# A matmul with rotary embedding on one core: the lower rows follow the upper rows at 1024 columns, in another order of the banks

## The chip, the cores and the metric

One core of one Trainium2 chip. TensorE (PE) multiplies and transposes, VectorE (DVE), ScalarE (ACT) and GpSimd (POOL) work on tensors, and SyncE (SP), ScalarE and GpSimd issue DMA transfers. The metric is the device time of one execution in microseconds; less is better. Each engine works through its instructions in order and waits on semaphores that others raise.

## The reference

```
y = np.matmul(x, weight)                       # x: (16, 512, 768), weight: (768, 768)
y = y.reshape(batch, seq, n_heads, head_dim)   # 12 heads of 64
y1, y2 = y[..., :32], y[..., 32:]
out1 = y1 * cos1 - y2 * sin1                   # cos, sin: (512, 64), by place in the sequence
out2 = y2 * cos2 + y1 * sin2
out = np.concatenate([out1, out2], axis=-1).reshape(batch, seq, hidden)
```

All inputs and the output are float32. The kernel multiplies in float16 and accumulates in float32.

## The kernel before

**Tiles, pairs, groups.** The 8192 rows of `x` are 64 tiles of 128 rows. Four tiles make a group (`QB` = 4, 16 groups, `g`), two make a pair. A group takes the same places of the sequence from four batches, so that one slice of the cosine and sine table serves it. Its result has 4 x 768 = 3072 columns, and these lie in PSUM as `py`, six banks of 512 float32 columns (`ps0` to `ps5`). A pair has 1536 columns, three banks, and the border between its two tiles lies in the middle of the second of them.

**The way of a tile.** SyncE loads it (`load`, line 192), ScalarE casts it to float16 (`cast`, 227), TensorE transposes its six chunks of 128 x 128 into PSUM (`turn`, 235, or `turn_rows`, 247, which does it in two halves of 64 rows), and ScalarE copies that to SBUF as `xt` (the copy in the same function). From group 5 to 14 the second pair of each group comes another way: it is loaded as blocks (`load_quarter`, 200), by SyncE and then cast by ScalarE (`cast_pair`, 265), or by GpSimd's queue, which casts on the way, and VectorE transposes it (`turn_pair`, 273) into `xp`. The weight is loaded and cast once at the start.

**Upper and lower rows.** A tile's product needs six chunks of the contraction. In the groups 1 to 14 each chunk is split in two matmuls: one on the upper 64 rows of the TensorE array (`r` = 0) and one on the lower 64 (`r` = 1), which run at the same time. Both halves add into the same bank of PSUM. The function `steps` (330) cuts a tile into three steps of 256 output columns (six chunks, 1536 streamed columns); where a whole bank belongs to one tile, two steps are done as matmuls of 512 columns, three chunks each. `both` (359) puts a step `n` of the upper rows beside step `n - LAG` of the lower rows, with `LAG` = 3 (587), in the order of streamed columns. So the lower rows are one tile behind, and are in another bank. The upper rows' first matmul opens a bank (`start`), and the first lower one waits by semaphore for the upper rows' last in that bank (`closed`, `after`). When the lower rows have finished a bank, its rope is emitted.

**The rope.** `rope` (379) works on units of `units` (292). VectorE multiplies a unit's columns in PSUM by the cosines and by the sines and writes both products to SBUF (line 394); GpSimd adds them, with the halves of each head swapped in the second (410), to the output tile `ov`. In the groups 1 to 13 VectorE takes 512 columns and GpSimd 1024, two units together. The products lie in five buffers of 2 x 1024 columns: `tq` (three) and two in the memory of the raw weight, which is free after its cast. Group 0 has units of 1024 columns and is multiplied with all 128 rows (`mm_piece`, 319); so is the last group (15), which has three units of 512 and six of 256, of which VectorE adds the last two itself (`late`).

**Order.** All is written out by hand in the loop of line 605, tile by tile: the matmuls with their ropes, a transpose of a tile three ahead, the casts five ahead, GpSimd's loads twenty ahead, and the stores. `turns` and `casts` go in line with the other work of TensorE and ScalarE. A group's output is stored by two transfers that ScalarE issues after the first (`s` = 0) and the third tile (`s` = 2) of the next group (633 to 636). `Flow.do` (42) records for each instruction what it reads and writes, and puts in the semaphore waits that follow from it. After the loop's end the last group's pieces are stored, by SyncE and ScalarE.

Of the kernel before, what the change touches and what calls it, by code (L numbers as in the profile page):

```python
# [10 lines left out]
FP32 = mybir.dt.float32  # L11
# [94 lines left out]
def kernel(  # L106
# [37 lines left out]
    NX, NB, NBH, NC, NCP, NXT, NXP, NTQ, NOV = 10, 3, 3, 5, 2, 8, 4, 3, 4  # L144
# [14 lines left out]
    tq_b = [sbuf(f"tq{i}", [P, 2, 1024], FP32) for i in range(NTQ)]  # L159
    w_flat = w_raw.rearrange("p t e n -> p (t e n)")  # L160
    tq_b += [w_flat[:, ts(i, 2048)].rearrange("p (j n) -> p j n", j=2) for i in range(2)]
    W_HOME = [f"wr{t}{h}" for t, h in CHUNKS]
    ov_b = [sbuf(f"ov{i}", [P, QB * H], FP32) for i in range(NOV)]
# [128 lines left out]
    def units(g):  # L292
        if g == 0:
            return [(c, c + 1024, py[:, c : c + 1024], [f"ps{c // 512}", f"ps{c // 512 + 1}"], "pool")
                    for c in (0, 1024, 2048)]
        u = [(c, c + 512, py[:, c : c + 512], [f"ps{c // 512}"], "pool")
             for c in range(0, 3072 if g < LAST else 1536, 512)]
        if g == LAST:
            for k, (home, bank) in enumerate([
                (py[:, 1536:1792], "ps3"), (py[:, 0:256], "ps0"),  # L300
                (py[:, 2048:2304], "ps4"), (py[:, 2560:2816], "ps5"),
                (pt_b[0][:, 0:256], "pt0"), (pt_b[1][:, 0:256], "pt1"),
            ]):
                c = 1536 + 256 * k
                u.append((c, c + 256, home, [bank], "pool" if k < 4 else "dve"))
        return u
# [20 lines left out]

    closed = {}

    def steps(n, r):  # L330

        i, part = divmod(n, 3)
        g, s = divmod(i, QB)
        c0 = s * H + 256 * part
        bank, wide = c0 // 512, (s % 2 == 0 and part < 2) or (s % 2 == 1 and part > 0)
        lo = bank * 512 if wide else c0
        hi = lo + (512 if wide else 256)
        first, final = c0 % 512 == 0, c0 % 512 == 256
        chunks = (CHUNKS[:3] if first else CHUNKS[3:]) if wide else CHUNKS
        rows = ts(r, HP)  # L340
        get, key = xT[i]
        out_ = []
        for t, h in chunks:
            opens = r == 0 and first and (t, h) == chunks[0]
            shuts = final and (t, h) == chunks[-1]

            def go(t=t, h=h, opens=opens, shuts=shuts):
                after = closed[g, bank] if r and first and (t, h) == chunks[0] else 0
                do("pe", lambda eng: eng.matmul(  # L349
                    py[:, lo:hi], get(t, h)[rows], w_sb[rows, t, h, lo - s * H : hi - s * H],  # L350
                    start=opens, stop=r == 1 and shuts, skip_group_check=True),
                    reads=[key, f"w{t}{h}"], writes=[f"ps{bank}"], tick=shuts, after=after)
                if r == 0 and shuts:
                    closed[g, bank] = f.count["pe"]

            out_.append((hi - lo, go))
        return out_, (g, bank) if r == 1 and final else None

    def both(n, m):

        done, work = None, []
        for r, k in ((0, n), (1, m)):
            if k is None:
                continue
            mm, ended = steps(k, r)
            done = ended or done
            at = 0
            for cols, go in mm:
                work.append((at, r, len(work), go))
                at += cols  # L370
        for _, _, _, go in sorted(work, key=lambda w: w[:3]):
            go()
        return done
# [5 lines left out]
    def rope(g, u):  # L379
# [3 lines left out]
        half = 0 < g < LAST - 1  # L383
        if adder == "dve":
            k = len(late)
            tq, keys = xs_b[k][:, 0 : 2 * w].rearrange("p (j n) -> p j n", j=2), [f"xs{k}"]
        elif half and c0 % 1024:
            k = tq_of[0]
            tq, keys = tq_b[k][:, :, w : 2 * w], [f"tq{k}b"] + (W_HOME if k >= NTQ else [])
        else:  # L390
            k = tq_of[0] = ring("tq", NTQ + 2)
            tq = tq_b[k][:, :, 0:w]
            keys = [f"tq{k}a"] + [f"tq{k}b"] * (not half) + (W_HOME if k >= NTQ else [])
# [10 lines left out]
        if half:  # L404
            if c0 % 1024 == 0:
                return
            c0, w, tq, keys = c0 - w, 2 * w, tq_b[k], [f"tq{k}a", f"tq{k}b"]
# [179 lines left out]
    LAG = 3  # L587

# [16 lines left out]
    for i in range(QB, NTILE):  # L605
# [4 lines left out]
        if g < LAST:  # L610
            for n in range(3 * i, 3 * i + 3):
                done = both(n, n - LAG if n - LAG >= 3 * QB else None)
                if done:
                    rope(done[0], units(done[0])[done[1]])
                if n == 3 * i and i > QB + 1:
                    turns(i + T_AHEAD, 1)
        for n in range(3 * i - LAG, 3 * i) if i == QB * LAST else ():
            done = both(None, n)
            if done:
                rope(done[0], units(done[0])[done[1]])  # L620
# [12 lines left out]
        if s == 0 and g > 0:  # L633
            store(g - 1, 0, 2 * H, "act")
        if s == 2 and g > 0:
# [50 lines left out]
```

## Time and profile before

| | |
|---|---|
| median of 3 runs (range) | 154.4 us (154.16 to 154.4) |
| the profiled execution: its time | 154.73 us |
| its span, first to last instruction | 152.9 us |
| mean granted TensorE clock | 0.994 |
| a lower or upper 512-column matmul, by the modelled duration | 0.376 us, x672 |
| a 256-column one | 0.269 us, x672 |
| VectorE rope of 512 columns (x51 in `tq`) | 1.215 us |
| VectorE rope of 1024 columns (group 0) | 2.285 us |
| VectorE transposes of a pair | 0.969 and 1.235 us |
| ScalarE cast of a tile, copy of a transposed tile | 0.902 and 0.799 us |
| GpSimd add of 1024 columns | 2.373 us |

Matmuls are pipelined, so their durations overlap in one row half; the distance between their starts is what a matmul costs. The rope's shape is given in the profile as 128x1024 where it writes two products of 512 columns each. The chain of waits follows the last instruction back to what released it; an engine that is not on it costs nothing there. "py" is the product in PSUM, "pt" the PSUM of the transposes, "xc" a cast tile.

### The profile page before, as it was taken

The page shows a single profiled execution, that of the slowest core. Times are in us where ns is not written, and L with a number is a line of the kernel's source. Part 1 is how long each engine was busy: PE and PEld are TensorE (multiplying, and loading weights), DVE is VectorE, ACT ScalarE, POOL GpSimd, SP SyncE. Part 2 cuts the span into 40 slices and gives each one's busy share as a digit, 9 for nine tenths or more (in the row PEclk, how much of TensorE's full clock was granted, in tenths as well). Part 3 has the DMA queues.
Part 4 walks back from the last instruction along what each step waited for, and adds up shares of the span by engine and source line. Part 5 has one row for each costly group of instructions (what it writes and reads, how often), then busy time and mean ns, then how long its engine had stood idle before and what let it go on. Part 6 is the DMA issues. An engine that isn't in the chain of part 4 may idle for free.

```text
span 152.9 us, 4416 instructions
## 1 busy us (share of the span) xinstructions
PE 141.5 (93%) x1944; PEld 102.7 (67%) x1944; DVE 129.3 (85%) x119; ACT 78.7 (51%) x92; POOL 124.6 (81%) x81
## 2 busy tenths in 40 slices
PE   6669997999999999999999999999999999999930
PEld 2325674777777778777777777777777777766720
DVE  0244995888888999999999999999999999978980
ACT  3444778879778843556263726273526735461000
POOL 1000299599999999999999999999997979799970
PEclk9999999999999999999999999999999999999997
DMA  3999999999999999999999999999999998550992
GB/s 124 350 395 404 400 402 385 385 380 257 363 358 352 368 336 353 349 400 340 339 341 392 364 336 339 372 370 334 345 360 407 416 403 323 233 210 0 374 354 97
DMA packets 27555, 51.27 MB, mean 335 GB/s; under 512 B 7184, under 2 KB 13072, under 8 KB 27536
## 3 DMA queue, kind: packets, MB, share of 16 engines
q1 hardware_dynamic: 13504, 24.78, 46.8%
q10 hardware_dynamic: 8592, 24.25, 40.3%
q0 software_dynamic: 5440, 1.97, 10.4%
q8 instruction: 15, 0.25, 0.6%
q14 instruction: 4, 0.03, 0.1%
HBM read 27.79 MB, written 25.17 MB: 346 GB/s over the span
## 4 chain that ended last, share of the span: by engine, by line
PE 86%; DMA 5%; DVE 3%; SPq 1%; ACT 1%; issue 1%; DVEq 0%
PE py L349 72%; PE py L324 8%; DMA w_raw<-in_weight_dram 5%; PE pt L257 4%; PE pt L242 1%; DVE w_raw L394 1%; SPq L196 1%; DVE ov L410 1%; SPq L218 1%; ACT xc L176 1%; ACT xt L176 1%; DVE xs L394 0%; DVE w_sb L176 0%; DVE tq L394 0%; DVEq L57 0%
## 5 line engine op out<-in xcount | busy, mean ns | idle before, releaser
L349 PE MATMUL py<-w_sb,xt 64*128 64x512 f16 (+1 forms) x864 | 95.6, 323 | 0.0
L410 POOL TENSOR_TENSOR ov<-tq 128x1024 f32<-128x1024 f32 (+2 forms) x33 | 68.9, 2109 | 19.3 <-DVE tq L394 19.1
L394 DVE TENSOR_TENSOR tq<-py,csn 128x1024 f32<-128x1024 f32 (+2 forms) x56 | 68.1, 1253 | 3.6 <-PE py L349 3.1
L349 PEld LDWEIGHTS py<-w_sb,xt 64*128 64x128 f16 x864 | 58.8, 94 | 17.2
L349 PE MATMUL py<-w_sb,xp 64*128 64x512 f16 (+1 forms) x480 | 61.9, 323 | 0.0
L176 ACT COPY xt<-pt 128x768 f16<-128x768 f16 x42 | 33.5, 799 | 39.4 <-PE pt L257 27.3
L176 ACT CAST xc<-xs 128x768 f16<-128x768 f32 x44 | 39.1, 902 | 21.1 <-DMA xs<-in_x_dram 17.2
L394 DVE TENSOR_TENSOR w_raw<-py,csn 128x1024 f32<-128x1024 f32 (+1 forms) x38 | 45.3, 1191 | 5.3 <-PE py L349 3.7
L410 POOL TENSOR_TENSOR ov<-w_raw 128x1024 f32<-128x1024 f32 (+2 forms) x22 | 44.3, 2027 | 3.4 <-DVE w_raw L394 3.2
L349 PEld LDWEIGHTS py<-w_sb,xp 64*128 64x128 f16 x480 | 35.5, 94 | 9.9
L324 PE MATMUL py<-w_sb,xt 128*128 128x256 f16 (+1 forms) x96 | 15.5, 313 | 1.9 <-DVE w_sb L176 1.7
L257 PEld LDWEIGHTS pt<-ident,xc 64*128 64x128 f16 x432 | 13.7, 95 | 2.7 <-ACT xc L176 1.4
L324 PEld LDWEIGHTS py<-w_sb,xt 128*128 128x128 f16 x96 | 8.7, 98 | 7.5 <-DVE w_sb L176 3.2
L257 PE MATMUL pt<-ident,xc 64*128 64x64 f16 x432 | 12.6, 190 | 1.1 <-ACT xc L176 1.1
L211 POOL DMA_DIRECT2D xh<-in_x_dram x20 | 11.7, 594 | 0.0
L176 ACT CAST xd<-xb 128x1536 f16<-128x1536 f32 x5 | 8.2, 1630 | 1.5 <-DMA xb<-in_x_dram 1.4
L176 DVE CAST w_sb<-w_raw 128x768 f16<-128x768 f32 x6 | 3.4, 560 | 4.4 <-DMA w_raw<-in_weight_dram 4.4
L285 DVE STREAM_TRANSPOSE xp<-xh 128x768 f32<-128x768 f32 x5 | 6.2, 1235 | 0.0
L492 PE MATMUL py<-cold 128*128 128x512 f16 x12 | 4.3, 518 | 1.4 <-DVE cold L435 1.4
L176 DVE COPY xt<-pt 128x768 f16<-128x768 f16 x2 | 1.1, 557 | 4.9 <-PE pt L242 4.9
L285 DVE STREAM_TRANSPOSE xp<-xd 128x768 f32<-128x768 f32 x5 | 4.8, 969 | 0.0
L242 PEld LDWEIGHTS pt<-ident,xc 128*128 128x128 f16 x48 | 3.0, 98 | 2.7 <-ACT xc L176 1.8
(16 smaller groups left out, 13.2 us busy)
## 6 DMA issues: line engine op xcount, KB each, us to landing
out_dram<-ov ACTq DMA_DIRECT2D x30, 768.0 KB, 8.8
xs<-in_x_dram SPq DMA_DIRECT2D x44, 384.0 KB, 15.9
xb<-in_x_dram SPq DMA_DIRECT2D x20, 192.0 KB, 18.0
w_raw<-in_weight_dram SPq DMA_DIRECT2D x6, 384.0 KB, 7.8
xh<-in_x_dram POOLq DMA_DIRECT2D x20, 96.0 KB, 13.7
out_dram<-ov SPq DMA_DIRECT2D x1, 384.0 KB, 3.1
out_dram<-ov ACTq DMA_DIRECT2D x1, 384.0 KB, 2.8
out_dram<-ov SPq DMA_DIRECT2D x1, 256.0 KB, 2.1
```

What stands on the lines that cost most here:

```text
L176: eng.copy(out=o, in_=i_) if e == "act" else eng.tensor_copy(out=o, in_=i_)
L196: do(e, lambda eng: eng.dma_start(out=xs_b[k], in_=x[b].rearrange("(p r) h -> r p h", r=SB)[r]), writes=[f"xs{k}"], dma=f"xs{k}")
L211: do(e, lambda eng: eng.dma_start(out=dst[ts(q, R)], in_=src[r, q]), writes=[f"{name}q{q}"], dma=name)
L218: do(e, lambda eng: eng.dma_start(out=w_raw[:, t, h], in_=wv[t, h]), writes=[f"wr{t}{h}"], dma=f"w{t}{h}")
L242: do("pe", lambda eng: eng.transpose(pt[:, t, h, :], src[:, t, h, :], ident), reads=[f"xc{c}", "ident"], writes=[f"pt{k}"], tick=(t, h) == ...
L257: do("pe", lambda eng: eng.transpose(pts[r][:, t, h, :], src[rows, t, h, :], ident[rows, rows]), reads=[f"xc{c}", "ident"], writes=[f"pt{r ...
L285: do("dve", lambda eng: eng.transpose(out=dst, in_=src), reads=rd, writes=[f"xp{z}"])
L324: do("pe", lambda eng: eng.matmul(ps, get(t, h), w_sb[:, t, h, a - s * H : z - s * H], start=start, stop=stop), reads=[key, f"w{t}{h}"], w ...
L349: do("pe", lambda eng: eng.matmul(py[:, lo:hi], get(t, h)[rows], w_sb[rows, t, h, lo - s * H : hi - s * H], start=opens, stop=r == 1 and s ...
L394: do("dve", lambda eng: eng.tensor_tensor(out=tq.rearrange("p j (h d) -> p j h d", d=D), in0=ps.rearrange("p (h d) -> p h d", d=D) .unsque ...
L410: do(adder, lambda eng: eng.tensor_tensor(out=ov_b[o][:, ds(c0, w)].rearrange("p (h t d) -> p h t d", t=2, d=HD), in0=tq[:, 0].rearrange(" ...
L492: do("pe", lambda eng: eng.matmul(py[:, ts(b, 512)], cold[:, 0:P], cold, start=True, stop=warmed[0] < WARM - 6), reads=["cold"], writes=[f ...
```

## The change

The upper rows take a pair's three banks in the order 0, 1, 2 as before. The lower rows now take them in the order 2, 0, 1, and start 1024 streamed columns (two matmuls of 512) behind the upper rows (`LAG` = 1024), not one tile. Bank 2 is therefore opened by the lower rows and closed by the upper ones, the banks 0 and 1 the other way round. A bank's columns are done for all six chunks before the next, and the middle bank in two parts of 256 columns. `walk` yields this order for a pair and one half of the rows, `one` emits a matmul, and the new `both` merges the two lines by their streamed columns. The pair's second tile is so needed by the lower rows 1024 columns after the pair begins.

A rope is emitted when all of its banks have been finished by both halves. In the groups 1 to 14 a pair has a unit of 512 columns (its first bank) and one of 1024; GpSimd adds 1536 columns at once in the groups 1 to 13. The buffers of the products are one memory of 6144 columns and the raw weight's 4608, cut by `products` into three homes for a pair's 2 x 1536 columns, into three of 2 x 1024 for group 0 and six of 2 x 512 for the last group. Stores of the groups 0 to 13 are issued one tile later in the next group; those of group 14 are where they were.

```diff
+    tq_mem = sbuf("tq", [P, 6144], FP32)
+    def products(at, n, lo, hi):
+        mem, base, name = (tq_mem, at, "tq") if at < 6144 else (w_flat, at - 6144, "tw")
...
+    HOMES0, HOMES, HOMESL = (0, 2048, 4096), (6144, 0, 3072), (0, 1024, 2048, 3072, 4096, 5120)
...
+        if g < LAST:
+            return [(c, z, py[:, c:z], [f"ps{b}" for b in range(c // 512, z // 512)], "pool")
+                    for c, z in ((0, 512), (512, 1536), (1536, 2048), (2048, 3072))]
...
-    LAG = 3
+    LAG = 1024
...
+    def walk(pair, r):
+        g, h = divmod(pair, 2)
+        for bank in ((0, 1, 2) if r == 0 else (2, 0, 1)):
+            opens = (r == 0) == (bank < 2)
+            lo = h * 1536 + bank * 512
+            parts = [(lo, lo + 512)] if bank != 1 else [(lo, lo + 256), (lo + 256, lo + 512)]
+            for a, z in parts:
+                i = g * QB + a // H
+                for c in CHUNKS:
+                    yield z - a, (g, i, a, z, r, c, opens,
+                                  opens and (a, c) == (lo, CHUNKS[0]),
+                                  c == CHUNKS[-1], z == lo + 512)
+    def one(g, i, a, z, r, c, opens, start, ends, whole):
+        s, rows, (t, h), bank = i % QB, ts(r, HP), c, a // 512
+        get, key = xT[i]
+        after = closed[g, bank] if not opens and c == CHUNKS[0] else 0
+        do("pe", lambda eng: eng.matmul(
+            py[:, a:z], get(t, h)[rows], w_sb[rows, t, h, a - s * H : z - s * H],
+            start=start, stop=not opens and ends and whole, skip_group_check=True),
+            reads=[key, f"w{t}{h}"], writes=[f"ps{bank}"], tick=ends, after=after)
...
+    lines = [[], []]
+    at = [0, LAG]
+    def both(upto):
+        while True:
+            n = [(at[r], r) for r in (0, 1) if lines[r]]
+            if not n or min(n)[0] >= upto:
+                return
+            r = min(n)[1]
+            cols, what = lines[r].pop(0)
+            at[r] += cols
+            one(*what)
...
-        if half:
-            if c0 % 1024 == 0:
+        if whole:
+            if c0 % 1536 == 0:
                 return
-            c0, w, tq, keys = c0 - w, 2 * w, tq_b[k], [f"tq{k}a", f"tq{k}b"]
+            c0, w = c0 - 512, 1536
+            tq, keys = products(tq_of[0], 1536, 0, 1536)
...
-            for n in range(3 * i, 3 * i + 3):
-                done = both(n, n - LAG if n - LAG >= 3 * QB else None)
+            if s % 2 == 0:
+                for r in range(2):
+                    lines[r].extend(walk(i // 2, r))
+            for n in range(1, 4):
+                both((i - QB) * 4608 + n * 1536)
...
+        if i == QB * LAST:
+            both(NTILE * 4608)
...
-        if s == 0 and g > 0:
+        late_by = 1 if g < LAST else 0
+        if s == late_by and g > 0:
             store(g - 1, 0, 2 * H, "act")
-        if s == 2 and g > 0:
+        if s == 2 + late_by and g > 0:
             store(g - 1, 2 * H, 4 * H, "act")
```

## The prediction

> **What bounds the kernel now.** I read the busy shares first, then the chain of waits, then the timelines of its two ends.
>
> ```profile
> PE 141.5 (93%) x1944; PEld 102.7 (67%) x1944; DVE 129.3 (85%) x119; ACT 78.7 (51%) x92; POOL 124.6 (81%) x81
> ...
> PE 86%; DMA 5%; DVE 3%; SPq 1%; ACT 1%; issue 1%; DVEq 0%
> ```
>
> TensorE carries 86% of the chain. In order of time the chain shows which parts of it matter:
>
> ```profile
> 18.98 2.01 PE py L349 x12
> ...
> 23.42 0.80 ACT xt L176
> 24.22 0.80 ACT xc L176
> 25.02 0.05 issue
> 25.07 0.35 PE pt L257 x12
> ...
> 66.59 1.95 PE py L349 x18
> 68.53 0.18 PE pt L257 x12
> 68.71 5.85 PE py L349 x56
> ...
> 136.31 2.05 PE py L349 x12
> 138.36 2.06 PE py L324 x12
> ...
> 147.76 0.98 DVE ov L410 x2
> ```
>
> From 25.07 us to the last group nothing but TensorE is on the chain: 1.95 us of matmuls for each tile of 768 columns, 8.15 us for a group of four tiles with two transposed ones. Before that there is one stall, in which ScalarE makes a copy and a cast while TensorE waits (1.07 us in the PE timeline). At 136.31 stand twelve matmuls of the lower rows alone: the upper rows have finished. The ends of the other engines:
>
> ```profile
> 15.83 6.69 DVE L394 TENSOR_TENSOR tq<-py,csn 128x2048 f32<-128x2048 f32 x3
> ...
> 19.50 0.80 ACT L176 COPY xt<-pt 128x768 f16<-128x768 f16 x1
> 21.30 0.80 ACT L176 COPY xt<-pt 128x768 f16<-128x768 f16 x1 [0.99 <-PE pt L257]
> 21.99 0.91 ACT L176 CAST xc<-xs 128x768 f16<-128x768 f32 x1
> ...
> 24.12 1.69 ACT L176 CAST xc<-xs 128x768 f16<-128x768 f32 x2
> ```
>
> The three ropes of group 0 run without a break until 22.5 us, and ScalarE is the second chain of the start.
>
> **The drain of the lower rows (gain).** Lower rows now trail by 1024 columns, not by three steps of 1536. A 512-column matmul starts 0.216 us after the one before in its rows, a 256-column one 0.109 us (starts in the trace). Twelve matmuls alone are 6 x 0.216 + 6 x 0.109 = 1.95 us (2.05 on the chain); what is left alone now is four of 256, 0.44 us. That is **-1.51 us**, in full, as the last group's matmuls need both halves of the rows. Bounds: -1.61 by the chain's 2.05, -1.45 if the start of the last group hides a weight load.
>
> **The start (loss).** Earlier the lower rows' first bank opened after tile 4 had been done by the upper rows. Now the lower rows open bank 2 after three upper matmuls of tile 4, with columns of tile 5. That needs tile 5's transposed copy (ScalarE, 19.50 to 20.30) and bank 2 free from group 0's second rope (15.83 + 2.21 + 2.28 = 20.32 us by the starts in the trace). The fourth upper matmul, due at 19.59, stands behind this wait in TensorE's order and starts near 20.40: **0.81 us late**. Behind it are tile 6's transposes, for which ScalarE waits (21.30 before), and then its copy, tile 7's cast, tile 7's copy and tile 8's cast, whose end releases the stall at 25.07. Through this serial chain the delay passes on. If both halves keep step, tile 6's copy starts at 22.05 and tile 8's transposes at 25.78: +0.71. The lower half starts its stream 512 columns behind, though; if the transposes wait for that half (0.216 us more), they are at 26.03: +0.96. Later in the start, tile 9's transposes need tile 8's copy, which ends within 0.05 us of when TensorE gets there. From then on TensorE had no slack to absorb it. I take **+0.85**, between 0.6 and 1.0. The store that ScalarE issued at 22.94 moves a tile later and saves nothing: the copy behind it waited for TensorE until 23.40.
>
> **The body (nothing).** Matmuls are the same number and widths, and upper and lower rows are in different banks at every moment of the new order, as before, so I leave 1.95 us a tile. What could stall it:
> - The first lower matmul of bank 0 waits for the upper one that closes this bank. A semaphore rises 0.395 us after the start of a 512-column matmul, 0.285 after a 256-column one (trace). The distance is 1536 columns (0.65 us) in bank 0 and 1280 (0.54 us) in bank 1; the weight load that carries the wait goes a matmul ahead, at 0.43 and 0.32 us. That leaves 0.04 us before the load is late and some 0.15 before the matmul is. Price 0; 56 such waits at 0.05 would be +2.8.
> - Bank 5 is opened by the lower rows 0.43 us into a pair, earlier than now, and read by a 1024-column rope (2.28 us, the row of group 0) behind a DVE transpose (1.24 us) in the ten groups with block pairs. From a group's start: its second pair begins at 4.08 us, the lower rows close bank 3 at 7.47 (7168 columns, a transpose and the semaphore), VectorE is at its rope until 8.6, at the transpose until 9.8 and at the long rope until 12.1. The next group needs the bank at 8.15 + 4.08 + 0.43 = 12.66, its weight load at 12.5. It fits by 0.4 us.
> - A pair's second tile is needed 0.43 us into the pair, not a tile later. ScalarE's copy must follow its transposes within about 2.3 us; the trace has one delay near it, a copy at 119.23 behind a pair's cast that had waited for a load, done 2.4 us after. At most 0.2 us.
>
> I take **0**, with 0 and +3 as ends (no gain is possible where TensorE never waits).
>
> **The work off the path.** VectorE's two 512-column units become one of 1024. By the starts a 512 unit takes 1.13 us of the engine and a 1024 unit 2.2, so a group saves 0.12 us of 6.8, hidden by TensorE's 8.15. GpSimd adds 1536 columns at once; no row has this, so I go on from these:
>
> ```profile
> L410 POOL TENSOR_TENSOR ov<-tq 128x1024 f32<-128x1024 f32 x26 | 61.2, 2373 | 19.3 <-DVE tq L394 19.1
> ...
> L410 POOL TENSOR_TENSOR ov<-tq 128x512 f32<-128x512 f32 x5 | 6.3, 1288 | 0.0
> ...
> L410 POOL TENSOR_TENSOR ov<-tq 128x256 f32<-128x256 f32 x2 | 1.4, 728 | 0.0
> ```
>
> A further 512 columns cost 1.085 us: 3.46 us (between 3.40 by the starts and 3.56 by proportion). Two make 6.9 a group where three took 7.0; with four input loads of 0.59 us in every second group that is 8.1 of 8.15 us, as now. These loads stand behind a longer add and go out some 1.1 us later, five groups ahead of use. The stores move a tile later on ScalarE's queue, because a 1536-column add ends late: the lower rows close the pair 4.7 us after the group's start, the rope ends at 7.0, the add at 10.4, or at 11.6 behind a set of loads. The stores are issued at 8.15 + 4.08 = 12.2, so they don't hold the copies behind them.
>
> **The tail (loss).** Call the end of the lower rows zero (138.36 now). VectorE's last rope of group 14 has 1024 columns and ends at 2.4 us, and GpSimd can only then add it, until 4.8. Behind that stand three adds of 512 (1.24 apart) and four of 256 (0.69 apart): the last begins at 10.5 and ends at 11.3, where it now ends at 9.75. VectorE itself catches up and ends as before. Now the last transfer is issued by SyncE at 10.8 and the end is at 13.0, 2.2 us later; the last one would be ScalarE's at 11.3. With 1.8 us (this store now) to 2.2 us to land: +0.1 to +0.5. Two of VectorE's late adds now run beside GpSimd's. The trace has one such case: the first late add, beside a GpSimd add, took 0.645 us, the second, alone, 0.411. Two late adds beside two GpSimd adds could cost 2 x 0.24 more. I take **+0.6**.
> The Trainium skill's page "SBUF — State Buffer" (section "SBUF: two separate sides") says that a VectorE instruction with two SBUF inputs and a GpSimd one exclude each other for their whole length. The 0.645 beside 0.411 agrees. By this rule both engines' last adds would take turns, as in the second rival below.
>
> **Sum.** -1.51 + 0.85 + 0 + 0.6 = -0.06 us. The profiled execution took 154.73 us (span 152.9 and 1.8 around it), 0.33 above the median of 154.4; so 154.67 for it and about **154.4** as a median.
>
> **Rivals.**
> 1. *The drain's gain is kept.* The start loses only 0.6 (both halves in step, ScalarE slightly earlier) and the tail 0.1 (no queueing of the stores, late adds not hindered): -0.8, 153.6; 152.9 if nothing is lost. For it: both sums are chains of short steps, any of which may have slack. Against: the wait at 20.32 is on two finished records, and GpSimd has no break in its last 9 us.
> 2. *GpSimd's end decides (slower).* Late adds and GpSimd's adds take turns in the last 2 us: 9.8 to 10.2, a GpSimd add, 10.8 to 11.2, the last GpSimd add to 11.9, a store to 13.9: tail +0.9 to +1.2 with +0.96 at the start gives +0.35 to +0.65, 154.8 to 155.1. It decides once GpSimd's last add ends later than 11.5 us after the lower rows.
> 3. *The body stalls (slower).* Bank 5's rope ends after 12.5 us from its group's start, each of ten groups loses what is over; half a microsecond more on VectorE (a late transpose) is +1 to +3, 155.5 to 157.5. For it: margins of 0.04 and 0.4 us, where the distance to the closing matmul is 512 columns (0.22 us) longer now and bank 5 is opened 2.2 us later in the pair. Against: no wait of TensorE on VectorE after 25 us now.
> 4. *The lag isn't what it says:* if waits for the closing matmul hold the lower rows back, the lag grows to what it was and the time with it: covered by 3.
>
> **How the numbers follow.** Forecast (gain given back, 153.9 to 154.8) 0.48; rival 1, 0.22; rival 2, 0.14; rivals 3 and 4, 0.16. What a measurement can tell from no change is 0.2%, 0.31 us. Of the forecast's 0.48, 0.11 falls below 154.09, 0.27 inside and 0.10 above 154.71. Faster 0.33, same 0.27, slower 0.40. The range leaves out the best of rival 1 and the worst of 3: 153.5 to 155.6; the forecast's own is 153.9 to 154.8.
>
> **What would show it.** Right: at the end some four matmuls of 256 by the lower rows alone; a TensorE wait for DVE near 19.6 to 20.4 us; tile 8's transposes between 25.7 and 26.1; 1.95 us a tile after that; GpSimd's last add 11 to 12 us after the lower rows. Wrong: TensorE waits for VectorE or itself between 30 and 130 us, or tile 8's transposes still at 25.1.

## The result, and the profile after

The changed kernel takes 155.84 us (median of 14 runs, 154.96 to 156.61) against 154.38 us before (14 runs): a ratio of 1.0102, 95% interval 1.0078 to 1.0126. It is slower by about 1.5 us (1.46 between the medians, 1.6 by the ratio), where 154.4 with a range up to 155.6 had been predicted. The profiled execution took 155.6 us, its span 153.8. All ratios are of fast runs; two of the profiled executions below are slow ones, those of e12_late3 (156.75 us, its median 154.79) and e16_mix_casts_late3 (155.62, its median 153.93).

Start-up moves from one execution to the next by up to 1.5 us; the first rope stands behind the tables' transfers. So every time below that compares two traces is counted from the **mark**, the end of group 0's second rope (20.32 us in the span of before, 19.77 in that of after). Up to there the two kernels do the same.

The page of the changed kernel: busy time and share of the span of each engine, the chain's shares, and the group of GpSimd's adds (busy us and mean ns of one; idle time before them and who ended it):

```profile
PE 141.6 (92%) x1944; PEld 103.0 (67%) x1944; DVE 126.1 (82%) x91; ACT 78.1 (51%) x92; POOL 122.8 (80%) x66
...
PE 69%; POOL 7%; DVE 6%; issue 5%; DMA 5%; SPq 4%; ACT 1%; POOLq 0%; DVEq 0%
...
L430 POOL TENSOR_TENSOR ov<-tq 128x1536 f32<-128x1536 f32 (+3 forms) x29 | 76.3, 2648 | 21.1 <-DVE tq L413 21.1
```

VectorE and GpSimd are busy for less time than before (126.1 and 122.8 us against 129.3 and 124.6), in fewer and longer instructions. But TensorE's share of the chain fell from 86% to 69%, and GpSimd, which was not on the chain at all, has 7%. The chain of waits in order of time (start, length, what) shows where:

```profile
15.29 4.50 DVE tq L413 x2
19.79 0.13 issue
...
128.69 1.15 DVE xp L294
129.84 2.18 DVE tq L413
...
132.16 1.04 POOL ov L430
133.20 2.40 issue
135.59 1.30 POOL ov L430 x2
...
143.93 2.49 POOL ov L430 x2
146.43 0.68 POOLq L660
147.11 2.41 POOL ov L430 x3
```

It begins with group 0's two ropes, as predicted, and runs over TensorE. But it leaves TensorE for VectorE some 10 us before the lower rows end (at 137.29 us), goes over a transpose and a rope of 1024 columns to GpSimd at 132.16, and stays there to the end. ("issue" between the adds is again GpSimd: its records are rough, and its adds follow one another.) GpSimd's timeline shows it as well. Its columns are start, length, line, operation, count, and in brackets the idle time before. First after, then before:

```profile
127.20 3.47 POOL L430 TENSOR_TENSOR ov<-w_raw 128x1536 f32<-128x1536 f32 x1
132.16 7.02 POOL L430 TENSOR_TENSOR ov<-tq 128x1536 f32<-128x1536 f32 x3 [1.49 <-DVE tq L413]
139.15 3.59 POOL L430 TENSOR_TENSOR ov<-w_raw 128x512 f32<-128x512 f32 x2
142.71 6.82 POOL L430 TENSOR_TENSOR ov<-tq 128x512 f32<-128x512 f32 x7
```

```profile
128.47 2.36 POOL L410 TENSOR_TENSOR ov<-tq 128x1024 f32<-128x1024 f32 x1
131.79 3.61 POOL L410 TENSOR_TENSOR ov<-tq 128x1024 f32<-128x1024 f32 x2 [0.96 <-DVE tq L394]
135.35 2.52 POOL L410 TENSOR_TENSOR ov<-w_raw 128x512 f32<-128x512 f32 x2
...
146.72 1.41 POOL L410 TENSOR_TENSOR ov<-w_raw 128x256 f32<-128x256 f32 x2
```

In both kernels GpSimd last pauses before group 13's last add and then works without a break to its end. After that pause it owes the same in both (the columns of the groups 14 and 15), and besides group 13's last add: 1024 columns before, 1536 now. That add begins at 111.47 us after the mark before and at 112.39 now, and is 1.1 us longer. Everything that GpSimd does later is late by about the sum. The measured balance, counted from the mark:

| | before | after | difference |
|---|---|---|---|
| tile 8's transposes | 4.75 | 5.80 | +1.05 |
| tile 61's transposes | 113.26 | 114.31 | +1.05 |
| the last group's first matmul | 117.97 | 117.51 | -0.46 |
| GpSimd's last add ends | 127.81 | 129.75 | +1.94 |
| the last store has landed | 131.02 | 132.31 | +1.29 |

### The profile page after: what moved, and what is told of

Its sections match the earlier page's. It is cut to its first block, busy times and chain, and to the rows that moved or that the text cites. A ratio compares the mean times of both kernels' runs of the same rounds, so it can differ in the third digit from the quotient of the medians.

```text
span 153.8 us, 4391 instructions
## 1 busy us (share of the span) xinstructions
PE 141.6 (92%) x1944; PEld 103.0 (67%) x1944; DVE 126.1 (82%) x91; ACT 78.1 (51%) x92; POOL 122.8 (80%) x66
## 4 chain that ended last, share of the span: by engine, by line
PE 69%; POOL 7%; DVE 6%; issue 5%; DMA 5%; SPq 4%; ACT 1%; POOLq 0%; DVEq 0%
PE py L361 65%; POOL ov L430 7%; DVE tq L413 5%; DMA sin_sb<-in_sin_dram 5%; PE pt L266 4%; SPq L227 2%; SPq L205 1%; DVE xp L294 1%; ACT xc L185 1%; POOLq L660 0%; SPq L467 0%; ACT xt L185 0%; DVE csn L557 0%; DVE csn L555 0%; DVEq L57 0%
## 5 line engine op out<-in xcount | busy, mean ns | idle before, releaser
L430 POOL TENSOR_TENSOR ov<-tq 128x1536 f32<-128x1536 f32 (+3 forms) x29 | 76.3, 2648 | 21.1 <-DVE tq L413 21.1
L361 PE MATMUL py<-w_sb,xt 64*128 64x256 f16 (+1 forms) x864 | 81.2, 323 | 1.1 <-DVE tq L413 0.7
L413 DVE TENSOR_TENSOR tq<-py,csn 128x2048 f32<-128x2048 f32 (+2 forms) x46 | 74.5, 1654 | 6.4 <-PE py L361 5.9
L361 PEld LDWEIGHTS py<-w_sb,xt 64*128 64x128 f16 x864 | 53.7, 94 | 18.7 <-DVE tq L413 1.2
L361 PE MATMUL py<-w_sb,xp 64*128 64x256 f16 (+1 forms) x480 | 46.8, 323 | 0.0
L413 DVE TENSOR_TENSOR w_raw<-py,csn 128x1024 f32<-128x1024 f32 (+1 forms) x20 | 35.0, 1749 | 5.5 <-PE py L361 4.8
L430 POOL TENSOR_TENSOR ov<-w_raw 128x1536 f32<-128x1536 f32 (+2 forms) x11 | 34.9, 3175 | 4.8 <-DVE w_raw L413 4.8
L361 PEld LDWEIGHTS py<-w_sb,xp 64*128 64x128 f16 x480 | 30.5, 94 | 9.4
L512 PE MATMUL py<-cold 128*128 128x512 f16 x12 | 5.5, 632 | 1.4 <-DVE cold L455 1.4
```

The lines of the kernel that those rows point to most:

```text
L361: do("pe", lambda eng: eng.matmul(py[:, a:z], get(t, h)[rows], w_sb[rows, t, h, a - s * H : z - s * H], start=start, stop=not opens and en ...
L413: do("dve", lambda eng: eng.tensor_tensor(out=tq.rearrange("p j (h d) -> p j h d", d=D), in0=ps.rearrange("p (h d) -> p h d", d=D) .unsque ...
L430: do(adder, lambda eng: eng.tensor_tensor(out=ov_b[o][:, ds(c0, w)].rearrange("p (h t d) -> p h t d", t=2, d=HD), in0=tq[:, 0].rearrange(" ...
L512: do("pe", lambda eng: eng.matmul(py[:, ts(b, 512)], cold[:, 0:P], cold, start=True, stop=warmed[0] < WARM - 6), reads=["cold"], writes=[f ...
```

## The experiments

All kernels are the changed kernel with the edits shown. Times are in us from the mark in the profiled execution, ratios are to before. "Tile 8" is the start of its transposes, "last group" that group's first matmul. Late loads tells by how much TensorE fell back against before between the transposes of tile 12 and those of tile 61; where that was over 0.1 us, a cast of ScalarE was waiting for its input load there. The trace columns are of one execution each, the ratios of 5 to 14.

| | ratio, 95% interval | tile 8 | last group | late loads | GpSimd ends | landed |
|---|---|---|---|---|---|---|
| before | 1 | 4.75 | 117.97 | 0 | 127.81 | 131.02 |
| after | 1.0102 [1.0078, 1.0126] | 5.80 | 117.51 | 0 | 129.75 | 132.31 |
| e1_split13 | 1.0048 [1.0022, 1.0074] | 5.80 | 117.53 | 0 | 129.22 | 131.72 |
| e2_lag2048 | 1.0131 [1.009, 1.0172] | 5.32 | 117.86 | 0.3 | 130.07 | 132.74 |
| e3_no_late | 1.0085 [1.0057, 1.0112] | 5.75 | 117.47 | 0 | 129.33 | 132.18 |
| e4_casts | 1.0084 [1.0052, 1.0117] | 5.06 | 116.94 | 0 | 129.15 | 131.84 |
| e5_start | 1.0115 [1.0069, 1.0162] | 4.93 | 118.72 | 1.6 | 130.60 | 133.77 |
| e6_tail512 | 0.9984 [0.9955, 1.0013] | 5.76 | 117.87 | 0.3 | 127.62 | 131.05 |
| e7_units_alone | 1.0108 [1.0067, 1.0149] | 4.75 | 117.97 | 0 | 129.67 | 132.10 |
| e8_both | 0.9966 [0.994, 0.9993] | 5.07 | 118.43 | 1.5 | 128.19 | 131.35 |
| e9_tail512 | 1.005 [0.9998, 1.0102] | 5.77 | 117.96 | 0.4 | 128.64 | 131.88 |
| e10_tail_casts | 1.0004 [0.9951, 1.0056] | 5.07 | 117.81 | 0.8 | 128.30 | 131.57 |
| e11_old_lag_tail | 1.0133 [1.0079, 1.0187] | 4.71 | 118.89 | 1.0 | 129.41 | 132.60 |
| e12_late3 | 0.9998 [0.9949, 1.0047] | 5.07 | 119.76 | 2.8 | 129.73 | 133.18 |
| e13_mix | 0.9989 [0.995, 1.0028] | 5.79 | 118.57 | 1.0 | 128.74 | 131.60 |
| e14_mix_casts | 0.9969 [0.9936, 1.0002] | 5.05 | 117.22 | 0.3 | 127.39 | 130.25 |
| e15_old_lag_mix | 1.0002 [0.9973, 1.0031] | 4.69 | 117.91 | 0 | 127.79 | 131.00 |
| e16_mix_casts_late3 | 0.9973 [0.9945, 1.0] | 5.07 | 118.96 | 2.0 | 128.52 | 132.35 |

### e1_split13: group 13's adds one by one

```diff
-        whole = 0 < g < LAST - 1
+        whole = 0 < g < LAST - 2
```

> Group 13's second pair is added as 512 and 1024 columns and not as 1536 (group 13 treated as group 14 is). Theory A (GpSimd's queue is unbroken from group 13's last unit to the end, so its work from there on sets the end): the 512 part fits into the 1.49 us that GpSimd idles before 132.16, and 2.3 us are left of 3.4, so GpSimd's last add and the end come 1.0 to 1.1 us earlier than in the changed kernel: ratio to before about 1.003. Theory B (the time was lost at the start, and the tail follows TensorE's end): no change, ratio 1.010.

Measured: 1.0048, 0.8 us less than the changed kernel by the medians' ratios. The GpSimd timeline of this run:

```profile
130.96 7.29 POOL L430 TENSOR_TENSOR ov<-tq 128x512 f32<-128x512 f32 x4
138.19 1.29 POOL L430 TENSOR_TENSOR ov<-w_raw 128x512 f32<-128x512 f32 x1
140.05 2.37 POOL L430 TENSOR_TENSOR ov<-w_raw 128x1024 f32<-128x1024 f32 x1 [0.57 <-DVE w_raw L413]
142.37 6.82 POOL L430 TENSOR_TENSOR ov<-tq 128x512 f32<-128x512 f32 x7
```

The first 512 columns of group 13's last pair are now added while VectorE is still at the other 1024. GpSimd's end moves forward by 0.53 us only, because the next obstacle appears: at 140.05 it has to wait 0.57 us for VectorE's 1024-column rope of group 14. Only GpSimd's adds differ from the changed kernel here, not VectorE's ropes, so the gain is GpSimd's queue; a second long unit stands behind the first.

### e2_lag2048: a lag of 2048 columns

```diff
-    LAG = 1024
+    LAG = 2048
```

> The lower rows trail by 2048 columns and not 1024. Theory A (the lower rows are one line of work that can't begin before tile 5's copy and group 0's second rope are ready, near 20.4 us, whatever the lag): the wait in the start shrinks by 0.43 us, what the lower rows do alone at the end grows by 0.43, the end of the lower rows stays where it is and so does the time: ratio 1.010. Theory C (the drain is a gain of its own and the stall in the start a loss of its own that is partly absorbed): 0.43 us slower at the end against less than 0.43 back at the start, ratio 1.011 to 1.013.

Measured: tile 8's transposes 0.48 us earlier than in the changed kernel, the last group 0.35 us later. The sum is -0.48 (start), +0.43 (1024 columns more to drain), +0.39 lost late in the body to an input load. The time, 1.0131, does not differ from the changed kernel's beyond the intervals. By the trace, what the start gives the drain takes: start stall and drain are one exchange, as the lower rows can't begin before the mark. The time alone would fit either theory.

### e3_no_late: without VectorE's two late adds

```diff
-        add()
+        if k > 9:
+            add()
         store(LAST, c, c + 256, "sp")
```

> The two adds of the last 512 columns that VectorE makes itself at the end are left out (these columns of the last tile are stored without them). Theory A with mutual exclusion: the two GpSimd adds beside them fall from 0.900 to about 0.69 us, GpSimd ends 0.4 us earlier after the lower rows' end, and the time falls by 0.3 to 0.6 us, ratio 1.007. Without exclusion: the GpSimd adds keep their 0.900 us and the time falls by no more than 0.1.

Measured: GpSimd's last adds are no longer hindered. Two of the four took about 0.90 us in the changed kernel where the others took 0.7; without VectorE's adds its end comes 0.42 us earlier. The landing gains only 0.13; the last stores are issued closer together. The ratio, 1.0085, is not told apart from 1.0102. The turn-taking is real and is the small part of the loss.

### e4_casts: tile 8's cast ahead of tile 7's copy

```diff
     turns(6)
+    casts(8)
...
-        casts(i + 1 + (C_AHEAD if i >= SETTLED else 3 if i == QB else 4), 1 + i % 2)
+        casts(i + 1 + (C_AHEAD if i >= SETTLED else 4), 1 + i % 2)
```

> ScalarE casts tile 7 before the main loop and tile 8 at the end of tile 4, one tile earlier each, so that tile 8's cast is ready when its transposes come. Theory A (a delay at the start goes through to the lower rows' end and to GpSimd's queue): tile 8's transposes come about 0.8 us earlier and so does everything after them, ratio 1.005. Theory D (GpSimd's work at the end swallows what TensorE gains): no change, ratio 1.010.

Measured: tile 8's transposes 0.74 us earlier, 0.64 in the body, 0.60 at GpSimd's end, 0.47 at the landing; the ratio, 1.0084, is not told apart from 1.0102. In the trace the start reaches the end of the kernel, through GpSimd, at most of its price (its add after the last pause begins at 111.78, the changed kernel's at 112.39), and still the kernel is slower than before although its last group begins 1.03 us earlier than before's. So the start is not the whole loss.

### e5_start: a first pair of the lower rows in an order that needs no free bank 2

For the first pair the rows exchange their order and the lag is 2048 columns.

```diff
-    LAG = 1024
+    LAG = 2048
...
+        if pair == 2:
+            for bank, half in (((0, 0), (2, 0), (1, 0), (1, 1)) if r == 0 else ((1, 0), (0, 0), (2, 0), (1, 1))):
...
```

> In the first pair alone the lower rows begin with the half of bank 1 that belongs to tile 4, then take bank 0, bank 2 and the rest of bank 1, and the upper rows go 0, 2, 1; the lag is 2048 columns throughout. So nothing of tile 5 is needed before about 20.3 us. Theory A (start): no stall of the fourth upper matmul; tile 8's transposes come 4.75 us after the end of group 0's second rope, as in the kernel before (5.80 in the changed kernel); the lower rows end 1.05 - 0.43 = 0.6 us earlier than in the changed kernel, GpSimd's queue starts that much earlier and the time falls by 0.6 us, ratio 1.006. Theory B (the stall in the start is the whole loss): ratio 1.000 to 1.002.

Measured: the stall of the start is gone (4.93), but the time is 1.0115. In the profiled execution TensorE lost 1.6 us at tile 53, where the copy that it waited for stood behind a cast that waited 4.1 us for its load, and VectorE's first late add took 2.80 us. A miss for the expectation; as that loss is larger than what the start gained, the run doesn't tell what a better start is worth.

### e6_tail512 and e8_both: 512-column units in the last two groups

In these two runs the ropes and adds of the second pairs of the groups 13 and 14 are left out, so their times are those of less work. e8_both has the earlier cast of e4_casts besides.

```diff
-        if g < LAST:
+        if g < LAST - 2:
...
-        whole = 0 < g < LAST - 1
+        whole = 0 < g < LAST - 2
```

> Groups 13 and 14 have units of 512 columns, multiplied and added one by one; the rest is as in the changed kernel. Theory A: GpSimd gets work earlier in both groups: from group 13's last unit it has one add of 512 (1.24 us) instead of 3.4 us, and the last unit of group 14 is ready 1.1 us earlier; it does 0.3 us more work in group 14. Its last add and the end come 1.2 to 1.5 us earlier after the lower rows' end than in the changed kernel, ratio 1.001 to 1.003. Theory B (the start alone): no change, 1.010.

> The casts of the fourth experiment and the short units in groups 13 and 14 together. Theory A: both gains add, 0.6 and 1.2 to 1.5 us: ratio 0.996 to 0.999, a version at or below the kernel before. If the loads of the input limit the body when TensorE starts earlier, the first of them is lost: 1.001.

Measured: 0.9984 and 0.9966. They show that with GpSimd and VectorE relieved in the tail the new order runs no slower than before; they say nothing on the size of what short units bring. e9_tail512 and e10_tail_casts are these two runs with the work complete.

### e7_units_alone: new units and stores, old order and lag

```diff
-    LAG = 1024
+    LAG = 4608
...
-        for bank in ((0, 1, 2) if r == 0 else (2, 0, 1)):
-            opens = (r == 0) == (bank < 2)
+        for bank in (0, 1, 2):
+            opens = r == 0
```

> The changed kernel with the order of banks and the lag of the kernel before (0, 1, 2 in both halves, 4608 columns): units, adds and stores are the new ones. Theory A (the tail of long units is the loss; the new lag wins at the end what it loses at the start and what GpSimd swallows): tile 8's transposes at 4.75 us after group 0's second rope, the lower rows' end as in the kernel before, and still GpSimd's last add 11.5 to 12 us after it: ratio 1.007 to 1.011. Theory B (the new lag and order lose the time at the start): ratio 1.000 to 1.003.

Measured: 1.0108, as much as the whole change. TensorE is at before's times to 0.02 us in every tile, and GpSimd's last add ends 1.86 us late:

```profile
128.07 3.46 POOL L430 TENSOR_TENSOR ov<-w_raw 128x1536 f32<-128x1536 f32 x1 [0.56 <-DVE w_raw L413]
132.52 7.01 POOL L430 TENSOR_TENSOR ov<-tq 128x1536 f32<-128x1536 f32 x3 [0.99 <-DVE tq L413]
139.47 3.68 POOL L430 TENSOR_TENSOR ov<-w_raw 128x512 f32<-128x512 f32 x2
```

This is the run that splits the change. The longer units, with the later stores, cost as much as the whole change, and they cost it without delaying TensorE at any point: the 1536-column add after the last pause begins at 112.25 after the mark (before's at 111.47) and is 1.1 us longer. The new order and lag, with what they win at the drain and lose at the start, changed nothing that could be measured beside it.

### e9_tail512, e10_tail_casts, e11_old_lag_tail, e12_late3: short units in groups 13 and 14

```diff
-        if g < LAST:
+        if g < LAST - 2:
...
-             for c in range(0, 1536, 512)]
+             for c in range(0, 3072 if g < LAST else 1536, 512)]
...
-        whole = 0 < g < LAST - 1
+        whole = 0 < g < LAST - 2
```

e10_tail_casts adds the cast of e4_casts, e11_old_lag_tail the order and lag of e7_units_alone. e12_late3 is e10_tail_casts with one more late add on VectorE:

```diff
-                u.append((c, c + 256, home, [bank], "pool" if k < 4 else "dve"))
+                u.append((c, c + 256, home, [bank], "pool" if k < 3 else "dve"))
```

> The changed kernel with the groups 13 and 14 in six rope units of 512 columns each, added one by one by GpSimd; nothing is left out. Theory A (the loss is GpSimd's queue, which has no break from group 13's last 1536-column add to the end, because long units make an add begin late): group 13's last add begins about 1.2 us earlier against the lower rows' end and is 1.3 us long instead of 3.5, GpSimd's last add ends 1.5 to 2.2 us earlier against the lower rows than in the changed kernel, and the time is 0.996 to 1.001 of before. Theory B (the later start and not the tail makes it slow): tile 8's transposes stand 1.05 us late as in the changed kernel and the time stays at 1.008 to 1.012.

> The short units of the groups 13 and 14, and besides tile 8's cast moved ahead of tile 7's copy on ScalarE, which brought tile 8's transposes 0.65 to 0.75 us forward in an earlier run. If TensorE's end and GpSimd's last adds both follow TensorE now: 0.5 to 0.7 us less than with the short units alone, 0.992 to 0.997 of before. If the casts that wait for their loads near 96 us after group 0's ropes take the lead back: as with the short units alone, 0.996 to 1.001.

> The changed kernel's units and later stores with the short units in the groups 13 and 14, but the old order of the banks and the old lag of 4608 columns. If the long units of these two groups are the whole loss of the change: 0.998 to 1.002 of before, with TensorE at before's times to 0.1 us and GpSimd's last add within 0.3 us of before's. If the longer units or later stores cost something elsewhere too: 1.005 or more. Against the run with the new order and the same tail it shows what the new order and lag are worth: -0.3 us by the ends of the lower rows, none if GpSimd's queue takes it.

> As the run with short units and the earlier cast, and VectorE adds the last three pieces of 256 columns instead of two. If GpSimd's queue still sets the end: its last add ends 0.7 us earlier and the time is 0.2 to 0.5 us less than without, 0.990 to 0.995 of before. If VectorE's and GpSimd's last adds take turns: VectorE's three late adds take 0.6 to 0.9 us each instead of 0.41, its end moves 0.7 us later and the time is the same or up to 0.3 us more.

Measured: 1.005, 1.0004, 1.0133 and 0.9998, with intervals of half a per cent to each side. e9_tail512 returns 1.11 us of GpSimd's 1.94. Its timeline tells why not all:

```profile
118.74 3.46 POOL L430 TENSOR_TENSOR ov<-tq 128x1536 f32<-128x1536 f32 x1
123.19 3.47 POOL L430 TENSOR_TENSOR ov<-tq 128x1536 f32<-128x1536 f32 x1 [0.99 <-DVE tq L413]
126.60 3.76 POOL L430 TENSOR_TENSOR ov<-w_raw 128x512 f32<-128x512 f32 x3
130.30 7.46 POOL L430 TENSOR_TENSOR ov<-tq 128x512 f32<-128x512 f32 x6
```

The last pause is now a group earlier, in front of group 12's last 1536-column add. From there GpSimd is busy without a break, 12 adds of 512 columns at 1.235 us for the two groups, and has no slack to catch up. The same obstacle, one group up. e11_old_lag_tail was a miss: I expected 0.998 to 1.002. Its profiled execution lost 1.0 us to a late load, and its queue has the same unbroken start; both together are the 1.6 us by which it lands late. Whether the missed time was the loads or the queue was open after this run. e12_late3 can't be told from e10_tail_casts by time.

### e13_mix to e16_mix_casts_late3: group 12's last adds short as well

The edit of e9_tail512, with the second pair of group 12 added as it comes (512 and 1024 columns):

```diff
-        whole = 0 < g < LAST - 1
+        whole = 0 < g < LAST - 2 and (g, c0 // 1536) != (LAST - 3, 1)
```

e14_mix_casts adds the earlier cast, e15_old_lag_mix the old order and lag, e16_mix_casts_late3 the cast and the third late add.

> The changed kernel with short units of 512 columns in the groups 13 and 14 and with the second pair of group 12 added as it comes, 512 and 1024 columns; nothing is left out. Theory A (GpSimd's queue from the last long add sets the end): group 12's last add ends 0.9 us earlier, and GpSimd's last add ends 0.7 to 1.0 us earlier against group 0's last rope than with the short units alone (127.6 to 128.0 us after it; 127.80 before, 129.75 in the changed kernel, 128.65 with the short units alone). The time is 0.998 to 1.002 of before, if no input load is late. Theory B (something else in the body or the start costs as much): GpSimd's last add moves as said, and the time stays at 1.005 or more.

> As the run with group 12's second pair added as it comes, and tile 8's cast moved ahead of tile 7's copy. Tile 8's transposes 5.1 us after group 0's second rope (5.8 without), TensorE and GpSimd 0.4 to 0.6 us earlier to the end, 0.994 to 0.998 of before; where a late input load takes the lead back, as without the earlier cast.

> The changed kernel's units and later stores with the same short adds from group 12's second pair on, but the old order of the banks and the old lag of 4608 columns. If the long units cost nothing but the tail: TensorE at before's times to 0.1 us, GpSimd's last add within 0.3 us of before's, 0.999 to 1.003 of before. If long adds or later stores delay input loads in the body: tile 32 to 40's transposes 0.5 us or more late and 1.005 or more.

> As the run with group 12's second pair added as it comes and the earlier cast, and VectorE adds the last three pieces of 256 columns, not two. GpSimd's last add ends 0.5 to 0.7 us earlier; the time is 0.1 to 0.4 us less than without, 0.992 to 0.997 of before, if VectorE's own end (its last rope, then three adds of 0.41 us and the first one longer) does not take over; if it does, the same as without.

Measured: 0.9989, 0.9969, 1.0002 and 0.9973. e15_old_lag_mix is the cleanest one (its expectation counts tiles among those that TensorE transposes; 32 to 40 are the tiles 44 to 60): with 1536-column adds in all groups up to 11 and in the first pair of group 12, but short ones behind that, every point of it stands where it stands in before: the last group at 117.91 (117.97), GpSimd's end at 127.79 (127.81), the landing at 131.00 (131.02). So long adds and later stores cost nothing in the body, and the loss of e7_units_alone lay in its long units from group 12's second pair on. e11_old_lag_tail differs from this run in group 12's second pair alone, and by 1.3% in time; in the traces 1.0 us of the difference is e11's late load, and the other 0.6 to 0.7 at GpSimd's end are the queue. Whether e11's other executions lost as much to loads is not known. The end of e15's chain of waits:

```profile
145.24 0.66 DVE xs L413 x2
145.90 0.46 issue
146.35 1.32 DVE ov L430 x2
```

GpSimd has left the end of the chain, which again goes to VectorE's ropes and late adds, as in before. Its queue has no break from 99.53 us after the mark on, longer than in e9_tail512 (103.96): what counts is where the queue ends, not its length. In e13_mix GpSimd's end was expected at 127.6 to 128.0 and came at 128.74; its profiled execution lost 0.97 us to a late load, without which it would have been near 127.8 (an estimate: 128.74 - 0.97). e14_mix_casts lands 0.77 us ahead of before and 2.06 ahead of the changed kernel. By time it clearly beats the changed kernel (0.9969 against 1.0102), and its lead on before, 0.3%, is at the edge of what its interval (0.9936 to 1.0002) can tell. The third late add of e16_mix_casts_late3 brought GpSimd's end closer to the last group's first matmul by 0.6 us, as expected (from 10.17 to 9.56), and VectorE's own end stayed at 10.5 behind that matmul and took over: no gain in time.

## Why the prediction was wrong

By its own terms, with the measured value of each, in us:

| step | predicted | measured |
|---|---|---|
| the drain | -1.51 | -1.51 (-0.46 at the last group, less the start's +1.05) |
| the start | +0.85 (0.6 to 1.0) | +1.05 |
| the body | 0 (0 to +3) | 0.00 |
| the tail | +0.6 (+0.1, and up to +1.2 in rival 2) | +1.75 (+1.29 at the landing, less -0.46) |
| sum | -0.06 | +1.29, and +1.5 to +1.6 by the timed runs |

**The drain was right.** TensorE's timeline of after shows the four 256-column matmuls of the lower rows alone that were forecast, where before had twelve matmuls:

```profile
136.31 0.51 PE L251 MATMUL pt<-ident,xc 128*128 128x128 f16 x6
136.75 0.61 PE L361 MATMUL py<-w_sb,xp 64*128 64x256 f16 x4
137.29 1.90 PE L336 MATMUL py<-w_sb,xt 128*128 128x512 f16 x10
```

**The start was right in kind, and 0.2 us too small.** The wait on VectorE stands where it was put, in front of the fourth matmul of tile 4's upper rows, and the delay passes along ScalarE's chain to tile 8 (TensorE's timeline of after):

```profile
19.91 1.67 PE L361 MATMUL py<-w_sb,xt 64*128 64x512 f16 x16 [0.70 <-DVE tq L413]
...
24.88 0.37 PE L361 MATMUL py<-w_sb,xt 64*128 64x512 f16 x1 [0.43 <-ACT xt L185]
25.58 0.35 PE L266 MATMUL pt<-ident,xc 64*128 64x64 f16 x12 [0.33 <-ACT xc L185]
```

Of the two cases that the prediction weighed, both halves in step or the lower one 512 columns behind, it was by its size the second, and 0.1 us over it: tile 8's transposes at 5.80 after the mark.

**The body was right.** The distance of the transposes from before's is 1.05 us at tile 8 and 1.05 at tile 61. The margins of 0.04 and 0.4 us that rival 3 feared held. The 1536-column add took 3.47 us (3.46 forecast).

**The tail was wrong.** The step that failed is "VectorE's last rope of group 14 has 1024 columns and ends at 2.4 us, and GpSimd can only then add it, until 4.8". The rope did end at 2.46 us after the lower rows (VectorE's timeline of after):

```profile
137.46 2.29 DVE L413 TENSOR_TENSOR w_raw<-py,csn 128x2048 f32<-128x2048 f32 x1 [0.62 <-PE py L361]
```

But GpSimd was not waiting for it: it came free at 3.09, still busy with what stood behind group 13's last 1536-column add, and the add ended at 5.45. I had counted the queue from that rope on and took GpSimd for idle before it; the pause that decides is a group earlier. The timeline of before showed this already: the prediction speaks of no break in GpSimd's last 9 us, and there is none in its last 16 (131.79 to 148.13). In the changed kernel group 13's last 1536 columns could not begin before VectorE had finished the pair's 1024-column rope, which itself stood behind a transpose of group 14's blocks (128.61 to 129.84). The rest adds up as follows: +0.65 from there, +0.30 from GpSimd adds that took turns with VectorE's late ones (last add ended at 12.24 instead of 11.3), and a last store that landed 2.54 us after its issue, where 1.8 to 2.2 had been taken. The last four stores were issued within 1.2 us, in before within 1.7; that this made the landing longer is not shown.

**Rival 2 had the outcome**, GpSimd's end decides, by its own condition: it was to decide once GpSimd's last add ended later than 11.5 us after the lower rows, and it ended at 12.24. It did not have the mechanism. Its tail of +0.9 to +1.2 was 0.55 to 0.85 us too low, for its price held only the turn-taking of the last 2 us, which e3_no_late put at 0.42 us. And the queue does not follow the lower rows' end: GpSimd's last pause ends 5.1 us before them (132.16 against 137.29). What the start loses comes ahead of that pause and reaches GpSimd's end at 0.60 for 0.74 us (e4_casts). e7_units_alone, which has neither the start's loss nor the drain's gain, ends its adds only 0.08 us earlier than the changed kernel. So of the 1.5 us that the shorter lag gains, GpSimd got some 0.8, an estimate (1.05 x 0.60 / 0.74 - 0.08), and the start took as much. Rival 1, the gain kept, needed a tail that was not bound by GpSimd; the same order with such a tail is e13_mix and e14_mix_casts, and there it is worth little: the new order against the old one with the same tail is 0.9989 against 1.0002, which the intervals don't separate.

The prediction named the page "SBUF — State Buffer" of the Trainium skill (section "SBUF: two separate sides") for the turn-taking of a VectorE instruction with two SBUF inputs and a GpSimd one. The runs agree: 0.90 us beside 0.7 on GpSimd, and more in the last section below.

**What stays open:** what makes an input load late in some executions (the column of late loads). It was not tried. It touches kernels with the old and the new order, and most of the runs that have the lead of the earlier cast. The runs e9 to e12 were taken together on one chip and all have it, those on other chips in part; whether the chip matters was not tried either.

## What to carry to other kernels

An engine that is 80% busy and not on the chain can still own the end of a kernel: look for its last pause and add up all that it owes from there, against the end that the main engine will have after the change. Longer instructions save fixed cost in the steady part (one rope of 1024 columns took 2.285 us, two of 512 took 2.43), but a consumer of a long unit starts when its last part is ready; so use short units for the last pairs before the end (here from three groups before), and undo each part of a change alone before believing that its largest number explains the result.

## What the runs showed of the hardware

**Turn-taking can hold a VectorE add for several GpSimd adds.** In before the two late adds of 256 columns took 0.98 us together. In e5_start they took 3.13: the first one, begun at 147.63, took 2.80 and ended only 0.28 us after GpSimd's unbroken row of adds (143.66 + 6.49 = 150.15). The first late adds of e9_tail512, e10_tail_casts and e11_old_lag_tail, which took 1.6 to 1.8 us, and that of before (0.645) also ended 0.27 to 0.29 us after GpSimd's last. VectorE's and GpSimd's timelines of e5_start:

```profile
147.63 3.13 DVE L441 TENSOR_TENSOR ov<-xs 128x256 f32<-128x256 f32 x2
```

```profile
143.66 6.49 POOL L441 TENSOR_TENSOR ov<-tq 128x512 f32<-128x512 f32 x7
```

In the changed kernel the late adds got their turn between GpSimd's adds (0.74 and 0.94 us), which then took 0.90. What decides between the two was not tried.

**The input loads have little slack in the body.** The busy time of each engine in three stretches of the changed kernel, with the granted clock, the mean share of 16 DMA engines and GB/s at the end of the row:

```profile
30.00:60.00 30.00, 30.00 (x488) 22.79 (x486) 25.74 (x16) 21.86 (x27) 27.13 (x16) 1.00 1.10 356
60.00:90.00 30.00, 30.00 (x444) 22.93 (x440) 28.46 (x19) 15.11 (x17) 29.41 (x16) 1.00 1.11 356
90.00:120.00 30.00, 30.00 (x452) 22.83 (x450) 28.49 (x19) 14.55 (x17) 28.29 (x13) 1.00 1.10 367
```

TensorE never pauses there, at full clock. The share of the DMA engines reads 1.10 to 1.11 in all three stretches, as it does in before; it is over 1, so it is not pure busy time, and that the DMA engines themselves are the limit is not shown. ScalarE's timeline of the changed kernel and then of e13_mix shows how late the loads come, at the cast that waits longest for one:

```profile
115.17 0.91 ACT L185 CAST xc<-xs 128x768 f16<-128x768 f32 x1 [3.54 <-DMA xs<-in_x_dram]
```

```profile
116.40 0.91 ACT L185 CAST xc<-xs 128x768 f16<-128x768 f32 x1 [3.95 <-DMA xs<-in_x_dram]
```

In the first TensorE was not held up; in the second, 1.50 us later from the mark, a copy behind this cast came late, and by tile 57 TensorE had lost 0.97 us. So a lead that TensorE wins at the start can be lost to a load some 80 to 100 us later, as in e5_start (1.6 us) and e8_both (1.5 us).
